# Encoder layer on one core: two sums of weight blocks added by the DMA queues, and eight fused pairs instead of six in three of four output groups

## The chip, the cores and the metric

The kernel runs on one core of a Trainium2 chip. A run's time is the device time of one execution, in microseconds (us). The profile comes from one execution, recorded by the hardware profiler. Its engines are TensorE (PE; the loading of its weights is PEld), VectorE (DVE), ScalarE (ACT), GpSimd (POOL) and SyncE (SP), each with an instruction queue of its own; DMAs are issued by SP, ACT or POOL.

## The reference, cut to what matters

One layer on 256 positions with 4096 channels: a normalised input times a wide matrix, a convolution path and an attention path beside each other, each with a gate, and an output projection whose result is added to the input.

```python
xn = rms_norm(x, norm_g)
h = xn @ w_in                                   # 4096 -> 14336
c_val, c_glu, c_gate, q, k, v, a_gate = split(h)
conv_out = conformer_conv(c_val, c_glu, ...) * silu(c_gate)
attn_out = longnet_mixture(rms(q), rms(k), v, rel_bias) * silu(a_gate)
mixed = concatenate([conv_out, attn_out])       # 256 x 4096
x = x + mixed @ w_out                           # 4096 -> 4096, the stage that changes
```

## The kernel before, in words

Every matrix product is made of three products in a 32-bit format of lower precision. Each operand is split into a high part (ScalarE rounds it) and a low part (VectorE subtracts the high part from the original). Then high x high, low x high and high x low are added up in PSUM. In the input stage these are L662, L663 and L665, in the output stage L782, L783 and L784 (in `triple`).

The work goes in groups of 1024 output columns: 14 input groups and four output groups (`og` 0 to 3). Along the inner dimension a group has 16 pairs `j`, each of two blocks `k` of 128 rows. The weights of a pair, 128 partitions x 2048 numbers, come by one DMA of 1 MB on SP's queue into one of three `raw` tiles (`load_pair`, L190). When the weights of pair `u` have been split, the load of pair `u + 3` is issued; SP waits until the slot is free.

An output group multiplies the mixed activations (256 rows, as two halves `s`) by two column halves `e`. A pair has therefore 2 x 2 blocks of activations, `a11` to `a22`, and 2 x 2 blocks of weights, `b11`, `b12`, `b21`, `b22`. There are two ways to work off a pair.

- A plain pair (`plain`) makes all 8 block products, each of 3 matmuls of 512 columns.
- A fused pair (`fused`) uses a Strassen-like scheme with 7 block products. It needs sums of blocks on both sides. On the activations these are `s1` to `s4`, made once (`mix_fuse`, called by `mix_split_gen`) and kept in a tile `mx` for all four groups. On the weights they are `t1` to `t4`, made anew for every pair in `split_fused`. The seven products go into `c11`, `c12`, `c21` and into `m1`, `m5`, `m6`, `m7`; the `m` banks are added to the output once per group (`add_more`).

`split_fused` has four steps. `one` makes the tile t13 = (t1, t3) on VectorE (L748) and splits b11 and b21. `two` rounds t13 on ScalarE (L732), starts t24 on VectorE (L759) and makes t13's low part (L736). `three` makes the other half of t24 (L765) and splits b22 (L767, L736). `four` splits t24. Each step asks for one or two tiles for its results. `before` lets steps run as long as no more than 8 such tiles are held, 10 after slot 10 of the first group, so the splits run ahead of TensorE by about that much.

The order of the pairs in a group is written out by hand:

```python
FUSED = (0, 1, 2, 3, 4, 5)
OUT_ORDERS = [(8, 9, 10, 0, 6, 1, 11, 2, 7, 3, 12, 4, 13, 5, 14, 15)]
OUT_ORDERS += 3 * [(8, 9, 0, 10, 1, 11, 2, 6, 3, 7, 4, 12, 5, 13, 14, 15)]
```

Pairs 0 to 7 are attention channels, 8 to 15 convolution channels. The convolution channels are multiplied by their gate late (L416), the last of them while the first output group already runs. `mix_split_gen` then splits or sums them (L547, L548, L559 to L571). All this side work is emitted by `pump`, step by step, with a budget of declared VectorE and ScalarE cost per call.

Tiles of 4 KB per partition share the pool tag `c4` with 15 slots: activations, gates, the `mx` tiles, t13, t24, the residual `xr` and split results beyond the eight `ws` slots. An instruction that writes such a tile waits until the slot's last user is done.

At the start seven small matmuls on a constant (`spin`, L900) run before the first weights have landed.

Of the kernel before, what the change touches and what calls it, by code (L numbers as in the profile page):

```python
# [17 lines left out]
P = 128  # L18
# [93 lines left out]
def layer_kernel(  # L112
# [17 lines left out]
    def t4(name):  # L130
        return sb.tile([P, 4, 256], F32, tag="c4", bufs=15, name=name)

# [44 lines left out]

    raw_tiles = {}

    def load_pair(j, cuts=(0, 2048), between=None):  # L180

        g, jj = divmod(j, n_pairs)
        if g >= NG:
            return
        if groups[g][0] == "out":
            jj = (OUT_ORDERS[g - n_in][jj] + n_pairs // 2) % n_pairs
        rt = sb.tile([P, 2048], F32, tag="raw", bufs=RAW, name=f"raw{j}")
        raw_tiles[j] = rt.rearrange("p (k c) -> p k c", k=2)
        for lo, hi in zip(cuts, cuts[1:]):
            nc.sync.dma_start(rt[:, lo:hi], w[g, jj, :, lo:hi])  # L190
            if between and hi == 1024:
                between()
# [335 lines left out]
    def mix_split_gen():  # L528
        waiting, done = list(OUT_ORDERS[0]), 0
        while waiting:  # L530
            for j in waiting:
                if 2 * j in mix_ready and 2 * j + 1 in mix_ready:
                    break
            else:
                yield
                continue
            while progress["in"] < done + 3:
                yield
            waiting.remove(j)
            done += 2  # L540
            if j in FUSED:
                yield from mix_fuse(j)
                continue
            for kk in (2 * j, 2 * j + 1):
                h, l = new_split(kk, "m")
                src = mix_ready[kk]
                nc.scalar.copy(h, src)  # L547
                nc.vector.tensor_sub(l, src, h.bitcast(F32))  # L548
                mh[kk], ml[kk] = h, l
                yield 335  # L550

    def mix_fuse(j):
# [4 lines left out]
        sums = t2(f"mix_sums{j}")  # L557
        s1, s2, s3, s4 = (sums[:, P * i : P * i + P] for i in range(4))
        nc.vector.tensor_add(s1, a21, a22)  # L559
# [5 lines left out]
        b0, b1 = new_split(2 * j, "m"), new_split(2 * j + 1, "m")  # L565
        more = sb.tile([P, 2, 512], F32R, tag="c4", bufs=15, name=f"mx{j}")
        parts = [[b[:, :P] for b in b0], [b[:, P:] for b in b0], b1]
        parts.append([more[:, i, : 3 * P] for i in range(2)])
        for (h, l), src in zip(parts, (a11, s1, a1, sums[:, P:])):
            nc.scalar.copy(h, src)  # L570
            nc.vector.tensor_sub(l, src, h.bitcast(F32))  # L571
            yield 300, 300
        names = {"a11": parts[0], "s1": parts[1]}
        names["a12"] = [b[:, :P] for b in b1]
        names["a22"] = [b[:, P:] for b in b1]
        for i in range(3):
            names[f"s{i + 2}"] = [more[:, hl, P * i : P * i + P] for hl in range(2)]
        mx[j] = names
# [93 lines left out]
    class Out:  # L672
# [3 lines left out]
        def __init__(self):  # L676
# [5 lines left out]
            for u in range((NG - n_in) * n_pairs):  # L682
                og, slot = divmod(u, n_pairs)
                j = OUT_ORDERS[og][slot]
                make = self.split_fused if j in FUSED else self.split_plain
                self.todo.extend((n, f, u) for n, f in make(u))

        def tile(self, name, of):
# [3 lines left out]
            self.tags.setdefault(of, []).append(tag)  # L692
            bufs = W_SLOTS if tag == "ws" else 15
            return sb.tile([P, 1024], F32R, tag=tag, bufs=bufs, name=name)
# [27 lines left out]
        def split_fused(self, u):  # L722
# [19 lines left out]
            def one():  # L742
                r = raw_tiles[n_in * n_pairs + u].rearrange("p k (e c) -> p (k e) c", e=2)
                kept["r"] = r
                t13 = kept["t13"] = t4(f"t13_{u}").rearrange("p a b -> p (a b)").rearrange(
                    "p (a c) -> p a c", a=2
                )
                nc.vector.tensor_sub(t13, r[:, 1:4:2, :], r[:, 0:2, :])  # L748
                h, l = both("b", r[:, 0:3:2, :])
                low(h, l, r[:, 0:3:2, :])  # L750
                keep(("b11", "b21"), h, l)

            def two():
                r, t13 = kept["r"], kept["t13"]
                t24 = kept["t24"] = t4(f"t24_{u}").rearrange("p a b -> p (a b)").rearrange(
                    "p (a c) -> p a c", a=2
                )
                h, l = both("t13", t13)
                nc.vector.tensor_sub(t24[:, 0, :], r[:, 3, :], t13[:, 0, :])  # L759
                low(h, l, t13)  # L760
                keep(("t1", "t3"), h, l)

            def three():
                r, t24 = kept["r"], kept["t24"]
                nc.vector.tensor_sub(t24[:, 1, :], r[:, 2, :], t24[:, 0, :])  # L765
                hl = halves("b22s", "b22")
                nc.scalar.copy(hl[:, 0, :], r[:, 3, :])  # L767
                low(hl[:, 0, :], hl[:, 1, :], r[:, 3, :])
                self.parts[(u, "b22")] = (hl[:, 0, :], hl[:, 1, :])

            def four():
                h, l = both("t24", kept["t24"])
                low(h, l, kept["t24"])
                keep(("t2", "t4"), h, l)
# [19 lines left out]
        def group(self, og):  # L794
# [3 lines left out]
            more = None  # L798
            fused_left = len(FUSED)
            for slot, j in enumerate(OUT_ORDERS[og]):  # L800
                u = og * n_pairs + slot
                self.settled |= slot == 10
                if slot == 9:
                    for e in range(2):
# [4 lines left out]
                        xr_tiles[(g, e)] = t  # L809
                if j in FUSED:  # L810
# [4 lines left out]
                    first, last = fused_left == len(FUSED), fused_left == 1  # L815
                    self.fused(u, j, one, more, first, last)
# [57 lines left out]
        def add_more(self, g, more):  # L874
# [8 lines left out]
            nc.vector.tensor_add(v, u, more["m7"])  # L883
            for dst, src in ((r[0][0], m1), (r[0][1], u), (r[1][0], v), (r[1][1], v)):
                nc.vector.tensor_add(dst, dst, src)

# [11 lines left out]
    spin = side("spin")  # L898
    for _ in range(7):
        nc.tensor.matmul(spin[:, :P], ones, ones, start=True, stop=True)  # L900
# [107 lines left out]
```

## Time and profile before

| | before |
|---|---|
| median of 3 runs | 1603.34 us (1603.1 to 1603.47) |
| the profiled execution, its time | 1603.12 us |
| its span, first to last instruction | 1601.3 us |
| mean granted TensorE clock | 0.998 |
| matmul rows | 6986 |
| busy: TensorE, VectorE, ScalarE, GpSimd | 1590.5, 1195.0, 968.2, 0.2 us |
| read from HBM | 318.08 MB |
| output groups in the span | 1257.76 us to the end |

A row of a timeline reads: start and length in us, engine, line of the kernel, operation, the tile written and the tiles read, shape, count. Brackets hold the idle time of the engine before it and what ended that. A row of waits reads: engine and line that waited, for whom; us in total, times, longest. A row of groups reads: line, engine, operation, tiles, shapes, count; busy us, mean ns of one; idle us before them. Matmul records overlap, so their pace is read from their starts, or from a count over a stretch.

### The profile page before, as it was taken

The numbers are of one execution on the slowest core, as the hardware profiler recorded it, in microseconds if no ns is written. First come the engines' busy times: TensorE is split into PE (matmuls) and PEld (weight loads), VectorE is DVE, ScalarE is ACT, GpSimd is POOL, SyncE is SP. The second block draws the span as 40 slices with busy tenths as digits, with TensorE's granted clock in tenths as the row PEclk, the third lists the DMA queues.
The fourth block names the chain that finished last, engine by engine and source line by source line (L and its number), as shares of the span: only waits on it lengthen the run. The fifth ranks groups of instructions, "written<-read, shape, count | busy, mean of one in ns | idle before, by whom it ended". The sixth has DMA issues, their size and how long they took to land.

```text
span 1601.3 us, 18984 instructions
## 1 busy us (share of the span) xinstructions
PE 1590.5 (99%) x6986; PEld 1312.8 (82%) x6986; DVE 1195.0 (75%) x1630; ACT 968.2 (60%) x1480; POOL 0.2 (0%) x4
## 2 busy tenths in 40 slices
PE   9999999999999999999999999999999999999999
PEld 7888888888888888888888888888878877888887
DVE  6668888888888887678755556555467889888886
ACT  6763534445453467755779557754789865545453
POOL 0000000000000000000000000000000000000000
PEclk9999999999999999999999999999999999999999
DMA  9755555555555555555555555455545556665653
GB/s 377 289 184 198 196 186 201 192 184 207 188 190 204 184 195 191 186 186 191 179 195 189 192 203 190 173 187 207 194 163 190 184 210 232 232 229 215 248 198 143
DMA packets 52892, 323.53 MB, mean 202 GB/s; under 512 B 5792, under 2 KB 8480, under 8 KB 16192
## 3 DMA queue, kind: packets, MB, share of 16 engines
q1 hardware_dynamic: 52512, 322.05, 56.4%
q8 instruction: 54, 0.88, 0.2%
q10 hardware_dynamic: 288, 0.28, 0.1%
q14 instruction: 38, 0.31, 0.1%
HBM read 318.08 MB, written 4.23 MB: 201 GB/s over the span
## 4 chain that ended last, share of the span: by engine, by line
PE 96%; ACT 1%; DVE 1%; issue 0%; DMA 0%; DVEq 0%; ACTq 0%
PE acc L662 25%; PE acc L663 25%; PE acc L665 25%; PE c L784 5%; PE c L782 5%; PE c L783 5%; PE m L784 1%; PE m L782 1%; PE m L783 1%; PE po L514 1%; PE psc L475 1%; ACT gate L315 0%; ACT pr L505 0%; DMA first_x<-in_x_cols_dram 0%; DVE t24l L736 0%
## 5 line engine op out<-in xcount | busy, mean ns | idle before, releaser
L205 DVE TENSOR_TENSOR wl<-raw,wh 128x1024 fp32r<-128x1024 f32 x447 | 546.9, 1224 | 336.9 <-ACT wh L204 335.9
L204 ACT CAST wh<-raw 128x1024 fp32r<-128x1024 f32 x447 | 469.6, 1052 | 434.9 <-PE acc L663 241.5
L662 PE MATMUL acc<-wh,xh 128*128 128x512 f32 x1792 | 703.8, 393 | 1.3 <-ACT xh L252 1.3
L663 PE MATMUL acc<-wh,xl 128*128 128x512 f32 x1792 | 698.4, 390 | 0.0
L665 PE MATMUL acc<-wl,xh 128*128 128x512 f32 x1792 | 483.7, 389 | 0.0
L662 PEld LDWEIGHTS acc<-wh,xh 128*128 128x128 f32 x1792 | 337.0, 188 | 72.3 <-ACT xh L252 1.6
L663 PEld LDWEIGHTS acc<-wh,xl 128*128 128x128 f32 x1792 | 336.8, 188 | 70.1 <-DVE xl L253 0.2
L665 PEld LDWEIGHTS acc<-wl,xh 128*128 128x128 f32 x1792 | 336.3, 188 | 70.3
L346 DVE SCALAR_TENSOR_TENSOR cT<-conv,wT,cT 128x241 f32<-128x241 f32 (+14 forms) x480 | 201.6, 471 | 0.0
L782 PE MATMUL c<-oh,mh 128*128 128x512 f32 x320 | 125.3, 391 | 0.5 <-ACT oh L716 0.5
L784 PE MATMUL c<-ol,mh 128*128 128x512 f32 x320 | 125.1, 391 | 0.5 <-DVE ol L717 0.5
L783 PE MATMUL c<-oh,ml 128*128 128x512 f32 x320 | 125.0, 391 | 0.0
L716 ACT CAST oh<-raw 128x1024 fp32r<-128x1024 f32 x80 | 83.2, 1051 | 50.8 <-PE c L783 34.4
L717 DVE TENSOR_TENSOR ol<-raw,oh 128x1024 fp32r<-128x1024 f32 x80 | 96.1, 1222 | 21.8 <-ACT oh L716 15.2
L505 ACT COPY pr<-turn_p 32x128 f32<-32x128 f32 x256 | 75.9, 297 | 9.2 <-DVE turn_p L499 5.7
L782 PEld LDWEIGHTS c<-oh,mh 128*128 128x128 f32 x320 | 60.5, 189 | 13.5 <-ACT oh L716 1.0
L784 PEld LDWEIGHTS c<-ol,mh 128*128 128x128 f32 x320 | 60.3, 189 | 13.5 <-DVE ol L717 1.0
L783 PEld LDWEIGHTS c<-oh,ml 128*128 128x128 f32 x320 | 60.5, 189 | 12.8
L732 ACT CAST t24h<-t 128x1024 fp32r<-128x1024 f32 x24 | 25.2, 1051 | 40.3 <-PE c L783 24.1
L736 DVE TENSOR_TENSOR t24l<-t,t24h 128x1024 fp32r<-128x1024 f32 x24 | 29.4, 1226 | 17.3 <-ACT t24h L732 17.3
L732 ACT CAST t13h<-t 128x1024 fp32r<-128x1024 f32 x24 | 25.3, 1053 | 18.2 <-DVE t L748 14.2
L732 ACT CAST bh<-raw 128x1024 fp32r<-128x1024 f32 x24 | 25.3, 1053 | 16.3 <-PE m L783 16.3
(195 smaller groups left out, 1030.8 us busy)
## 6 DMA issues: line engine op xcount, KB each, us to landing
raw<-in_w_dram SPq DMA_DIRECT2D x286, 1024.0 KB, 4.8
x<-in_x_dram SPq DMA_DIRECT2D x8, 512.0 KB, 7.4
xr<-in_x_dram SPq DMA_DIRECT2D x8, 512.0 KB, 6.0
out_dram<-xr SPq DMA_DIRECT2D x15, 256.0 KB, 2.9
xT<-in_x_cols_dram SPq DMA_DIRECT2D x7, 512.0 KB, 6.9
T<-bias_dram SPq DMA_DIRECT2D x16, 192.0 KB, 5.0
raw<-in_w_dram SPq DMA_DIRECT2D x3, 512.0 KB, 6.2
raw<-in_w_dram SPq DMA_DIRECT2D x2, 256.0 KB, 4.4
```

The source lines that it names most:

```text
L204: nc.scalar.copy(wh, src)
L205: nc.vector.tensor_sub(wl, src, wh.bitcast(F32))
L346: nc.vector.scalar_tensor_tensor(c[:, t, lo:hi], a[:, t, lo + sh : hi + sh], wT[:, ch, k : k + 1], c[:, t, lo:hi], op0=ALU.mult, op1=ALU.add,)
L505: nc.scalar.copy(dst[32 * b : 32 * b + 32, :, :, 3 - a, :], backwards(blocks[32 * a : 32 * a + 32, :, :, b, :]),)
L662: nc.tensor.matmul(a, hs, wp, start=k == 0, stop=False)
L663: nc.tensor.matmul(a, ls, wp, start=False, stop=False)
L665: nc.tensor.matmul(a, hs, wp, start=False, stop=k == KT - 1)
L716: nc.scalar.copy(h, src)
L717: nc.vector.tensor_sub(l, src, h.bitcast(F32))
L782: nc.tensor.matmul(acc, a[0], b[0], start=start, stop=False)
L783: nc.tensor.matmul(acc, a[1], b[0], start=False, stop=False)
L784: nc.tensor.matmul(acc, a[0], b[1], start=False, stop=stop)
```

## The change

- Groups two to four have eight fused pairs (0 to 7), the first group keeps six; the orders of groups two to four are new.
- The weight sums change sign, so that they are plain sums: t1 = b11 + b12, t3 = b12 + b22, t2 = t1 + b22, t4 = t2 + b21. The signs in `mix_sums` and `add_more` follow.
- t13 is no longer made by VectorE. `load_pair` loads (b11, b12) into the tile by SP and adds (b12, b22) to it by an accumulating DMA on POOL's queue. Block b12 is not loaded into `raw` for a fused pair; the rest of it comes by two DMAs.
- t24 is made in place in t13's tile, in the third step.
- All pairs get plain splits of their activations; the fused pairs' sums follow, those of pairs 6 and 7 after all the others. The declared costs in `mix_split_gen` change.
- The `c4` pool gets 18 slots instead of 15, and the scratch that the DMA queues of POOL reserve in each partition is set to 2048 bytes.
- Eleven spinning matmuls instead of seven.

```diff
-FUSED = (0, 1, 2, 3, 4, 5)
+FUSED = [range(6)] + 3 * [range(8)]
-OUT_ORDERS += 3 * [(8, 9, 0, 10, 1, 11, 2, 6, 3, 7, 4, 12, 5, 13, 14, 15)]
+OUT_ORDERS += 3 * [(8, 9, 0, 10, 1, 11, 2, 3, 12, 4, 5, 13, 6, 7, 14, 15)]
+C4 = 18
...
         rt = sb.tile([P, 2048], F32, tag="raw", bufs=RAW, name=f"raw{j}")
         raw_tiles[j] = rt.rearrange("p (k c) -> p k c", k=2)
+        if fuse:
+            src = w[g, jj].rearrange("p (k e c) -> p k e c", k=2, e=2)
+            t = sums[j] = t4(f"t13_{j}").rearrange("p a b -> p (a b)").rearrange(
+                "p (a c) -> p a c", a=2
+            )
+            nc.sync.dma_start(t, src[:, 0])
+            nc.gpsimd.dma_start(t, src[:, :, 1], accum_op=ALU.add)
+            nc.sync.dma_start(rt[:, 0:512], w[g, jj, :, 0:512])
+            nc.sync.dma_start(rt[:, 1024:2048], w[g, jj, :, 1024:2048])
+            return
...
-            if j in FUSED:
-                yield from mix_fuse(j)
-                continue
             for kk in (2 * j, 2 * j + 1):
                 h, l = new_split(kk, "m")
...
-                yield 335
+                yield 400, 400
+            if j in FUSED[0]:
+                yield from mix_sums(j)
+        for j in FUSED[-1]:
+            if j not in mx:
+                yield from mix_sums(j)
...
+        nc.vector.tensor_sub(s1, a21, a22)
         nc.vector.tensor_sub(s2, s1, a11)
-        yield 400
+        yield 580
         nc.vector.tensor_sub(s3, a11, a21)
-        nc.vector.tensor_sub(s4, a12, s2)
-        yield 400
+        nc.vector.tensor_add(s4, a12, s2)
+        yield 580
+        parts = sb.tile([P, 2, 512], F32R, tag="c4", bufs=C4, name=f"mx{j}")
+        nc.scalar.copy(parts[:, 0], t)
+        nc.vector.tensor_sub(parts[:, 1], t, parts[:, 0].bitcast(F32))
+        yield 690, 620
...
             def one():
-                nc.vector.tensor_sub(t13, r[:, 1:4:2, :], r[:, 0:2, :])
+                kept["r"], kept["t"] = r, sums.pop(j)
...
             def two():
                 h, l = both("t13", t)
-                nc.vector.tensor_sub(t24[:, 0, :], r[:, 3, :], t13[:, 0, :])
                 low(h, l, t)
...
             def three():
-                nc.vector.tensor_sub(t24[:, 1, :], r[:, 2, :], t24[:, 0, :])
                 hl = halves("b22s", "b22")
                 nc.scalar.copy(hl[:, 0, :], r[:, 3, :])
+                nc.vector.tensor_add(t[:, 0, :], t[:, 0, :], r[:, 3, :])
+                nc.vector.tensor_add(t[:, 1, :], t[:, 0, :], r[:, 2, :])
                 low(hl[:, 0, :], hl[:, 1, :], r[:, 3, :])
...
-    for _ in range(7):
+    for _ in range(11):
         nc.tensor.matmul(spin[:, :P], ones, ones, start=True, stop=True)
...
-    nc = _bacc.Bacc("TRN2", target_bir_lowering=False, num_devices=1)
+    nc = _bacc.Bacc("TRN2", target_bir_lowering=False, num_devices=1, dynamic_dma_scratch_size=2048)
```

More of the change, by code (lines that the diff above doesn't have):

```diff
@@ L549, in mix_split_gen, with mix_sums @@
                 mh[kk], ml[kk] = h, l
[L550 to L552 removed]
+                yield 400, 400
[4 more added lines that the diff above has]
+                yield from mix_sums(j)
+    def mix_sums(j):
         a0, a1 = mix_ready[2 * j], mix_ready[2 * j + 1]
         a11, a21, a12, a22 = a0[:, :P], a0[:, P:], a1[:, :P], a1[:, P:]
[L557 to L559 removed]
+        t = t2(f"mix_sums{j}")
+        s1, s2, s3, s4 = (t[:, P * i : P * i + P] for i in range(4))
+        nc.vector.tensor_sub(s1, a21, a22)
         nc.vector.tensor_sub(s2, s1, a11)
[L561 removed]
+        yield 580
         nc.vector.tensor_sub(s3, a11, a21)
[L563 to L577 removed]
+        nc.vector.tensor_add(s4, a12, s2)
[4 more added lines that the diff above has]
+        yield 690, 620
+        names = {
+            f"s{i + 1}": [parts[:, hl, P * i : P * i + P] for hl in range(2)] for i in range(4)
+        }
+        names["a11"] = [m[2 * j][:, :P] for m in (mh, ml)]
+        names["a12"] = [m[2 * j + 1][:, :P] for m in (mh, ml)]
+        names["a22"] = [m[2 * j + 1][:, P:] for m in (mh, ml)]
         mx[j] = names
@@ L771, in four @@
             def four():
-                h, l = both("t24", kept["t24"])
-                low(h, l, kept["t24"])
+                h, l = both("t24", kept["t"])
+                low(h, l, kept["t"])
                 keep(("t2", "t4"), h, l)
```

40 lines of the change are left out of this document (19 added, 21 removed).

## The prediction

> **What bounds the kernel now.** I read the page's head first, then the stages by windows, then TensorE's waits, then a timeline where it waits.
>
> ```profile
> PE 1590.5 (99%) x6986; PEld 1312.8 (82%) x6986; DVE 1195.0 (75%) x1630; ACT 968.2 (60%) x1480; POOL 0.2 (0%) x4
> ...
> 300.00:600.00 300.00, 300.00 (x1325) 248.43 (x1324) 255.27 (x415) 148.04 (x183) 0.00 (x0) 1.00 0.55 193
> ...
> 1257.70:1342.90 85.20, 81.61 (x344) 64.72 (x344) 75.59 (x104) 60.69 (x97) 0.00 (x0) 0.98 0.54 198
> 1348.30:1431.30 83.00, 83.00 (x368) 68.70 (x367) 72.19 (x78) 42.78 (x46) 0.00 (x0) 1.00 0.69 245
> ```
>
> The window rows read: stretch and its length, busy time and count of PE, of weight loads, DVE, ACT and POOL, then granted clock, DMA share and GB/s. TensorE is the bound: 1325 matmuls in 300 us without a gap, 0.2264 us each. So what TensorE need not do is gained, wherever it has no gap. The third row is nearly all of the first output group: 344 matmuls would take 77.9 us and took 85.2, so 7.3 us are lost there. The fourth row is the second group: 368 matmuls at that pace are 83.3 us, nothing is lost. The loss in the first group has a reason that the waits and a timeline show.
>
> ```profile
> PE m L782 <- ACT t24h L732: 1.2, 1, 1.2
> PE m L784 <- DVE t24l L736: 1.1, 3, 0.5
> ...
> 1281.57 1.22 DVE L748 TENSOR_TENSOR t<-raw 128x1024 f32<-128x1024 f32 x1
> ...
> 1290.20 1.23 DVE L736 TENSOR_TENSOR t24l<-t,t24h 128x1024 fp32r<-128x1024 f32 x1 [0.52 <-ACT t24h L732]
> ...
> 1290.22 0.50 PE L782 MATMUL m<-t24h,mx 128*128 128x512 f32 x1 [1.22 <-ACT t24h L732]
> ...
> 1292.75 0.63 PE L782 MATMUL c<-oh,mh 128*128 128x512 f32 x1
> 1293.18 0.63 PE L783 MATMUL c<-oh,ml 128*128 128x512 f32 x1
> ...
> 1293.00:1296.00 3.00, 3.00 (x9) 2.32 (x9) 3.00 (x4) 1.05 (x2) 0.00 (x0) 0.56 0.32 87
> ```
>
> TensorE waits for the last parts of a fused pair, t24, because VectorE (75.6 us busy of 85.2) is behind: from L748 at 1281.57 to the t24l at 1290.20 it works nearly without a gap, gate and mix work in between. The wait has a second price: right behind it matmuls start 0.43 us apart, and the granted clock is 0.56 in 1293 to 1296.
>
> **The change part by part.** The profiled execution took 1603.12 us (span 1601.3); the median is 1603.34, 0.22 above. The sum is made on 1603.12.
>
> *Matmuls.* A fused pair issues 7 products of 3 matmuls, a plain one 8 of 3. Fused pairs go from 6 in each of four groups to 6, 8, 8, 8: six more, 18 matmuls fewer, 18 x 0.2264 = 4.08 us. Groups two to four have no gap, so all of it counts: **-4.1**.
>
> *VectorE loses L748; the two t24 sums stay (now both in the third step, in place).*
>
> ```profile
> L736 DVE TENSOR_TENSOR t24l<-t,t24h 128x1024 fp32r<-128x1024 f32 x6 | 7.4, 1226 | 4.1 <-ACT t24h L732 4.1
> ...
> L748 DVE TENSOR_TENSOR t<-raw 128x1024 f32<-128x1024 f32 x6 | 7.3, 1218 | 0.0
> ...
> L759 DVE TENSOR_TENSOR t<-raw,t 128x512 f32<-128x512 f32 x6 | 4.1, 684 | 0.0
> ...
> L548 DVE TENSOR_TENSOR ml<-cT,mh 128x256 fp32r<-128x256 f32 x8 | 3.4, 422 | 0.5
> ...
> L571 DVE TENSOR_TENSOR mx<-mix_sums,mx 128x384 fp32r<-128x384 f32 x3 | 1.6, 541 | 0.5 <-ACT mx L570 0.5
> L571 DVE TENSOR_TENSOR ml<-mix_sums,mh 128x128 fp32r<-128x128 f32 x3 | 0.9, 290 | 1.1 <-ACT mh L570 1.1
> ...
> L559 DVE TENSOR_TENSOR mix_sums<-agv 128x128 f32<-128x128 f32 x2 | 0.6, 280 | 0.0
> ...
> 1282.70 1.22 DVE L736 TENSOR_TENSOR bl<-raw,bh 128x1024 fp32r<-128x1024 f32 x1
> ```
>
> These are VectorE's groups of the first output group. L748 costs 1.22 us, but the next operation starts 1.13 after it (1281.57 to 1282.70), so 1.13 is gained per fused pair: 6.8 us in the first group, 5.7 of it ahead of the last stall. Against it: the mix work. For a fused pair the low parts were two of 128 columns, one of 256, one of 384 (2 x 0.29 + 0.42 + 0.54 = 1.54); now they are two of 256 and one of 512 (2 x 0.42 + 0.68 = 1.52), and the four sums of 128 stay: nothing. But pairs 6 and 7, plain in the first group, now need sums as well: 2 x (4 x 0.28 + 0.68) = 3.6 us. They are emitted after all other mix work, behind the worst of it. Their pacing costs also rise (from 2000 to 2650 declared per fused pair), so some mix work moves from the input stage into this group. If VectorE paces this group, 7.3 us of loss fall by 5.7 less some 1 to 2 of moved mix work, and the slow-clock part (9 matmuls in 3 us around 1294 lack 1.0 us) goes with the wait that made it. Ends: 0 (ScalarE or the order of emission is late next) and -7.3. I take **-4.0**, nearer to VectorE's own count because the wait for t24h ends on it. Late next is t24l behind t24h, which already has 4.1 us of idle before it.
>
> In groups two to four two or three fused pairs in a row cost VectorE 3 lows of 1.13 and 3 halves of 0.6, 5.2 us, against 21 x 0.2264 = 4.75 of TensorE; each plain pair between gives 3 us back. Before, 6.3 and 5.4 alternated without a gap. Nothing, covered by the lead of the splits.
>
> *The sum t13 comes by two DMAs.* A load by SP, then, when it has landed, an accumulating one by POOL; ScalarE's t13h waits for the second. The raw load loses a quarter and splits in two. Per fused pair 1.75 MB replace 1 MB.
>
> ```profile
> raw<-in_w_dram SPq DMA_DIRECT2D x286, 1024.0 KB, 4.8
> x<-in_x_dram SPq DMA_DIRECT2D x8, 512.0 KB, 7.4
> xr<-in_x_dram SPq DMA_DIRECT2D x8, 512.0 KB, 6.0
> out_dram<-xr SPq DMA_DIRECT2D x15, 256.0 KB, 2.9
> ...
> SPq L190 <- DVE ol L717: 153.7, 35, 6.9
> SPq L190 <- DVE b22s L736: 105.2, 22, 7.9
> ...
> 1373.13 14.82 SPq L190 DMA_DIRECT2D raw<-in_w_dram  x4
> ...
> 1382.35 1.05 ACT L732 CAST bh<-raw 128x1024 fp32r<-128x1024 f32 x1 [1.48 <-PE m L783]
> ...
> 1383.63 1.05 ACT L732 CAST t13h<-t 128x1024 fp32r<-128x1024 f32 x1 [0.23 <-DVE t L748]
> ```
>
> A load of the second group is issued at 1373.13, as its slot comes free; its first cast is at 1382.35, its t13h at 1383.63, 10.5 us after issue. The new chain is a load (4.8 at most for this size) plus the accumulation A, which no row shows. Its nearest row is xr, 512 KB in the same shape: 6.0 (ends: 2.9, a quieter queue; 12, if reading the destination doubles it). 4.8 + 6.0 = 10.8 against 10.5. But SP waits about 4.5 us ahead of each load (153.7/35) for the raw slot alone, and the sum's own tile is not a raw slot, so its load, first of the pair's in SP's order, can go out right behind the pair before, up to those 4.5 us earlier. And the splits run ahead of TensorE, so a single delay is covered. I take **0**, plus **+0.3** for a few first uses. POOL has nothing else to do (0.2 us in all). SP issues two more DMAs per fused pair, under 1 us of its 4.5 of waiting.
>
> *Traffic.* Twelve slots with eight fused pairs last 8 x 4.75 + 4 x 5.43 = 59.7 us and load 18 MB of weights and 2 of residual and output: 21.0e6 bytes, 351 GB/s; 422 if accumulation counts double.
>
> ```profile
> 20.00:30.00 10.00, 10.00 (x45) 8.26 (x44) 7.24 (x10) 6.81 (x13) 0.00 (x0) 1.00 1.03 410
> ```
>
> At the start the queues carried 410 GB/s. So the plain count fits and the doubled one lacks 2 us in a group, which the four plain slots at its ends give back: 0. A rule of the Trainium skill (DMA: Bandwidth & Descriptors, Specifications) speaks against the change: it gives about 358 GB/s as a core's share of HBM. By that, the doubled count would need 70 us for 59.7. This trace's 410 is over it, so I stay with the row.
>
> *Eleven spins instead of seven.*
>
> ```profile
> 1.04 3.36 PE L900 MATMUL spin<-ones 128*128 128x128 f32 x14 [1.04 <-DVE ones L143]
> 5.73 0.80 PE L662 MATMUL acc<-wh,xh 128*128 128x512 f32 x1 [1.33 <-ACT xh L252]
> ...
> 8.13 0.63 PE L663 MATMUL acc<-wh,xl 128*128 128x512 f32 x1
> ...
> 8.90 0.39 PE L663 MATMUL acc<-wh,xl 128*128 128x512 f32 x1
> ...
> 14.39 1.05 ACT L204 CAST wh<-raw 128x1024 fp32r<-128x1024 f32 x1 [2.08 <-DMA raw<-in_w_dram]
> ...
> 16.86 0.39 PE L662 MATMUL acc<-wh,xh 128*128 128x512 f32 x1
> ```
>
> Seven spins are 14 rows, 0.24 us each; then 1.33 idle; then seven matmuls take 3.17 us (5.73 to 8.90) where 0.2264 each would be 1.58. Four more spins fill the gap: eight rows, 1.9 us, to 6.3 at the slow pace, a delay of 0.6. If the clock is granted by then, 1.6 are gained, of which ScalarE's cast at 15.44 (behind a DMA) lets some 1.4 through to the matmul at 16.86. Ends -1.4 and +0.6; I take **-0.9**, as the later gap and recovery at 1293 show that the clock follows how busy TensorE was. The Trainium skill (TensorE: Matmul & The Clock Gate, What's actually happening) says that full rate comes after one busy window of about 3.4 us whose phase is not the kernel's; by it, I estimate full rate between 4.5 and 7.9 us, and a gain near 0.8 after the delay. The trace agrees as far as 3.36 us of spins did not do it.
>
> *Smaller DMA scratch, 18 slots in c4, other signs.* Nothing by themselves: they make room, and the same number of adds remains.
>
> Sum: 1603.1 - 4.1 - 4.0 + 0.3 - 0.9 = 1594.4 for an execution as profiled, 1594.6 at the median.
>
> **The rivals.**
>
> *A: the accumulated sum is late (slower).* Three raw slots make a ring: load, accumulate, then t13h to the end of t24l.
>
> ```profile
> 1374.35 1.06 ACT L732 CAST t13h<-t 128x1024 fp32r<-128x1024 f32 x1 [1.15 <-PE c L784]
> ...
> 1378.89 1.23 DVE L736 TENSOR_TENSOR t24l<-t,t24h 128x1024 fp32r<-128x1024 f32 x1 [0.57 <-ACT t24h L732]
> ```
>
> That last part is 5.8 us. Two fused pairs and a plain one are 14.9 us on TensorE. The ring holds it up when 4.8 + A + 5.8 is over 14.9 + 4.5, the head start: A over 8.8 us. With A = 12, each round lacks 3.2, some four rounds in each of four groups, 51 us, less the splits' lead of up to 7.5 in each: about 20. 1594.6 + 20 = 1615. For it: accumulation has no row, and queues will be twice as full as in the 6.0. Against it: 6.0 is well under 8.8.
>
> *B: only the matmuls count.* The first group's loss stays because ScalarE's chain or the slower mix pacing takes VectorE's place: 1603.3 - 4.1 - 0.9 + 0.3 = 1598.6. For it: t24l waits for t24h there already. Against it: VectorE 89% busy in that window.
>
> *C: SP's queue stops in the first group.* The sum's load needs a c4 slot while gate, convolution and attention tiles still hold theirs; pairs 6 and 7 now hold an attention tile to the end of the mix work, and two of the three new slots go to their mix tiles.
>
> ```profile
> 1288.36 0.42 DVE L416 TENSOR_TENSOR cT<-cT,gate 128x256 f32<-128x256 f32 x1
> ...
> 1314.69 0.42 DVE L416 TENSOR_TENSOR cT<-cT,gate 128x256 f32<-128x256 f32 x1
> ```
>
> Between these two gate products none frees a tile, 26.3 us. A load that comes to a full pool half-way waits 13.2, and the raw loads behind it too; less 4.5 of head start, 8.7 are put back: 1603.3, no change. It decides from 16 or more tiles held at once. Against it: sums and splits free their own slots every pair.
>
> **How the numbers follow.** Forecast 0.56, its own range 1590 to 1597. B 0.17, A 0.17, C 0.10. Faster by over 0.2% (3.2 us, about what a measurement of this kernel can tell from no change) holds the forecast and nearly all of B: 0.73. Within: C, a mild A: 0.09. Slower: the rest of A and a bad C, 0.18. The low end, 1589.5, is the sum with the first group's whole 7.3 and 1.4 at the start gone (1590.5), and 1 us less for rounding in these; the high end, 1606, takes in B, C and the mildest of A (A of 9.5 us) and leaves its worse forms out.
>
> **What would show it.** Matmul rows are 6986 - 18 + 8 (spins) = 6976. L748 is gone; a POOL DMA appears 30 times, landing in about 6 us. The window of the first group shows under 4 us lost and no clock under 0.9; those of groups two to four PE busy throughout; the eighth matmul behind the spins starts before 8.5 us. Wrong would be: PE waits for t13h in groups two to four with ScalarE waiting for a DMA (A), SP waiting for the t load in the first group (C), or 7 us lost there still (B).

## The result and the profile after

The changed kernel takes 1628.65 us (median of four runs, 1625.05 to 1634.33) against 1603.33 us before: the ratio is 1.0161, 95% interval 1.0132 to 1.0191. (A ratio here is an estimate over all executions and need not be the quotient of the two medians.) It is 25 us slower, where 1594.6 was forecast; the range ended at 1606. The profiled execution took 1628.34 us with a span of 1626.5.

First the page's head, its DMA queues and its DMA issues.

```profile
PE 1599.4 (98%) x6976; PEld 1305.9 (80%) x6976; DVE 1191.2 (73%) x1634; ACT 974.4 (60%) x1488; POOL 33.1 (2%) x34
...
q1 hardware_dynamic: 61152, 329.92, 56.7%
q0 software_dynamic: 8160, 15.73, 5.7%
...
raw<-in_w_dram SPq DMA_DIRECT2D x33, 512.0 KB, 6.7
t<-in_w_dram SPq DMA_DIRECT2D x30, 512.0 KB, 7.8
t<-in_w_dram POOLq DMA_DIRECT2D x30, 512.0 KB, 7.9
```

The 6976 matmuls are those that were counted. The sum's two transfers land 7.8 and 7.9 us after their issue, in the median. Queue q0 holds the 30 accumulating DMAs and nothing else. Its 15.73 MB take 5.7% of the 16 engines' span, 0.36% for each MB; q1's 329.92 MB take 56.7%, 0.17% for each. So an accumulated byte occupies the DMA engines about twice as long as a loaded one: 170 GB/s of busy time (15.73 MB by 5.7% of 1626.5 us) against 358.

Then the four output groups by windows (length, busy and count of PE, weight loads, DVE, ACT and POOL, granted clock, DMA share, GB/s).

```profile
1257.26:1350.32 93.06, 87.63 (x368) 68.47 (x366) 78.25 (x114) 63.16 (x97) 6.82 (x7) 0.98 0.80 240
1350.32:1440.26 89.94, 85.49 (x361) 66.72 (x360) 70.03 (x77) 44.63 (x50) 8.76 (x8) 1.00 0.92 280
1440.26:1529.97 89.71, 85.26 (x362) 66.71 (x360) 70.01 (x77) 44.66 (x50) 8.75 (x8) 1.00 0.93 282
1529.97:1622.60 92.63, 85.95 (x361) 66.45 (x359) 69.36 (x77) 40.98 (x46) 7.67 (x7) 1.00 0.81 239
```

The first group issues 366 of these products, the others 360 (six fused pairs of 21 and ten plain ones of 24; then eight of each; a window's count holds one or two of its neighbour). At 0.2266 us each, measured between matmul starts in a stretch without gaps, that is 82.9 and 81.6 us. So the groups lose 10.1, 8.4, 8.1 and 11.1 us, 37.7 in all. The same count on the trace of before gives 7.6 in the first group and nothing in the others. There the first and the third group, of 366 products each, were:

```profile
1257.76:1348.33 90.57, 86.98 (x367) 69.20 (x366) 80.96 (x110) 62.42 (x99) 0.00 (x0) 0.98 0.53 194
...
1431.29:1514.25 82.96, 82.96 (x367) 68.69 (x366) 70.15 (x74) 43.04 (x46) 0.00 (x0) 1.00 0.63 228
```

All of the added time is here: +30.0 of gaps, -4.1 of matmuls, -0.5 ahead of the first group make +25.4, where the profiled executions differ by 25.2. "Losses" below always means this count, in the profiled execution.

What ends the gaps is in the waits (waiting engine, tile and line, what came last; total, times, longest).

```profile
DVE t13l L749 <- ACT t13h L745: 44.0, 18, 6.8
ACT t13h L745 <- DMA t<-in_w_dram: 35.2, 15, 6.0
...
PEld m L791 <- DVE t24l L749: 13.4, 15, 1.0
PEld m L791 <- DVE t13l L749: 7.0, 9, 1.0
...
PE m L789 <- ACT t13h L745: 4.5, 5, 1.1
...
SPq L198 <- PE c L790: 2.1, 5, 0.6
```

ScalarE's t13h waits for the sum's DMA 15 times. In 19 of the 30 fused pairs t13h starts within 0.1 us of its accumulation's landing. VectorE's low part, then TensorE, wait behind it. One such pair, the second of group two, in the timeline:

```profile
1351.83 3.07 SPq L621 DMA_DIRECT2D out_dram<-xr  x4
...
1354.94 0.53 SPq L198 DMA_DIRECT2D t<-in_w_dram  x1
1355.57 0.59 SPq L200 DMA_DIRECT2D raw<-in_w_dram  x1
...
1359.51 0.38 SPq L198 DMA_DIRECT2D t<-in_w_dram  x1
...
1362.58 1.11 POOL L199 DMA_DIRECT2D t<-in_w_dram  x1 [13.94 <-DVE ol L730]
...
1363.73 0.33 SPq L200 DMA_DIRECT2D raw<-in_w_dram  x1
...
1364.67 1.05 ACT L745 CAST bh<-raw 128x1024 fp32r<-128x1024 f32 x1 [2.22 <-DMA raw<-in_w_dram]
...
1372.70 1.04 ACT L745 CAST t13h<-t 128x1024 fp32r<-128x1024 f32 x1 [6.97 <-PE c L790]
...
1373.80 0.50 PE L789 MATMUL m<-t13h,mx 128*128 128x512 f32 x1 [0.88 <-ACT t13h L745]
1374.14 0.39 PE L790 MATMUL m<-t13h,mx 128*128 128x512 f32 x1
1375.06 0.50 PE L791 MATMUL m<-t13l,mx 128*128 128x512 f32 x1 [0.53 <-DVE t13l L749]
...
1377.11 0.50 PE L791 MATMUL c<-b22s,mx 128*128 128x512 f32 x1 [0.39 <-DVE b22s L749]
...
1378.90 0.50 PE L791 MATMUL m<-t24l,mx 128*128 128x512 f32 x1 [0.53 <-DVE t24l L749]
```

SP issues the load at 1354.94, behind the four stores of the output group just finished. POOL issues the accumulation at 1362.58, and it lands at 1372.62: 17.7 us from the first issue. ScalarE stands idle for 6.97 us ahead of t13h. The row names PE's release of the tile, but the cast starts 0.08 us behind the landing; the raw parts were there 8 us earlier (bh at 1364.67). Then each of the pair's parts comes late in turn: TensorE waits 0.88, 0.53, 0.39 and 0.53 us and starts matmuls 0.34 apart behind a wait. The pair loses 3.8 us; the same pair of the next two groups loses 3.5 and 3.9. These three make 11.2 of the 27.6 us that groups two to four lose; pairs 5 to 7, late in each group, make nearly all of the rest (16.2).

At the start, the extra spins bring TensorE's full pace forward:

```profile
1.06 4.27 PE L909 MATMUL spin<-ones 128*128 128x128 f32 x22 [1.06 <-DVE ones L144]
5.48 0.50 PE L675 MATMUL acc<-wh,xh 128*128 128x512 f32 x1 [0.16 <-ACT xh L266]
...
6.35 0.40 PE L675 MATMUL acc<-wh,xh 128*128 128x512 f32 x1
6.58 0.40 PE L676 MATMUL acc<-wh,xl 128*128 128x512 f32 x1
...
7.50 0.39 PE L676 MATMUL acc<-wh,xl 128*128 128x512 f32 x1
```

The first product starts at 5.48 (5.73 before) and the eighth at 7.50 (8.90 before).

### The profile page after: what moved, and what is told of

Read it like the earlier page. It is cut to its first block, busy times and chain, and to the rows that moved or that the text cites. A ratio compares the mean times of both kernels' runs of the same rounds, so it can differ in the third digit from the quotient of the medians.

```text
span 1626.5 us, 19221 instructions
## 1 busy us (share of the span) xinstructions
PE 1599.4 (98%) x6976; PEld 1305.9 (80%) x6976; DVE 1191.2 (73%) x1634; ACT 974.4 (60%) x1488; POOL 33.1 (2%) x34
## 3 DMA queue, kind: packets, MB, share of 16 engines
q1 hardware_dynamic: 61152, 329.92, 56.7%
q0 software_dynamic: 8160, 15.73, 5.7%
## 4 chain that ended last, share of the span: by engine, by line
PE 86%; DMA 7%; DVE 4%; ACT 2%; issue 1%; SPq 0%; ACTq 0%; DVEq 0%; POOLq 0%
PE acc L675 25%; PE acc L676 25%; PE acc L678 24%; DMA t<-in_w_dram 6%; PE c L789 3%; PE c L790 3%; PE c L791 3%; PE po L528 1%; PE psc L489 1%; PE m L791 1%; DVE t24l L749 1%; DVE t13l L749 1%; DMA raw<-in_w_dram 1%; ACT t24h L745 1%; DVE ol L730 1%
## 5 line engine op out<-in xcount | busy, mean ns | idle before, releaser
L791 PE MATMUL c<-ol,mh 128*128 128x512 f32 x272 | 106.0, 390 | 0.5 <-DVE ol L730 0.5
L789 PE MATMUL c<-oh,mh 128*128 128x512 f32 x272 | 106.0, 390 | 0.3 <-ACT oh L729 0.3
L790 PE MATMUL c<-oh,ml 128*128 128x512 f32 x272 | 105.9, 389 | 0.0
L730 DVE TENSOR_TENSOR ol<-raw,oh 128x1024 fp32r<-128x1024 f32 x68 | 80.5, 1219 | 4.8 <-ACT oh L729 3.3
L729 ACT CAST oh<-raw 128x1024 fp32r<-128x1024 f32 x68 | 68.5, 1047 | 19.3 <-PE c L790 8.8
L749 DVE TENSOR_TENSOR t13l<-t,t13h 128x1024 fp32r<-128x1024 f32 x30 | 36.7, 1222 | 44.0 <-ACT t13h L745 44.0
L199 POOL DMA_DIRECT2D t<-in_w_dram x30 | 33.0, 1098 | 1562.6 <-ACT gate L639 1255.9
L791 PEld LDWEIGHTS c<-ol,mh 128*128 128x128 f32 x272 | 51.1, 188 | 11.6 <-DVE ol L730 1.0
L789 PEld LDWEIGHTS c<-oh,mh 128*128 128x128 f32 x272 | 51.1, 188 | 11.4 <-ACT oh L729 0.7
L790 PEld LDWEIGHTS c<-oh,ml 128*128 128x128 f32 x272 | 51.1, 188 | 10.7
```

The costliest lines, as they stand in the source:

```text
L789: nc.tensor.matmul(acc, a[0], b[0], start=start, stop=False)
L790: nc.tensor.matmul(acc, a[1], b[0], start=False, stop=False)
L791: nc.tensor.matmul(acc, a[0], b[1], start=False, stop=stop)
```

## The experiments

Three theories were set against each other. L: the sum's load is issued too late, hardly ahead of the pair's own raw parts, and a chain of two transfers from there is too long. Q: the transfers themselves are too long, by the accumulation's price and by full queues, whenever they start. V: VectorE, in the order or the number of its mix operations. The first four kernels below shared one chip and its runs of the kernel before (median 1603.1), the next four another set (1603.43), the last two a third (1603.09). A loss belongs to one execution, which can lie off the median: 3.4 us above it for the copies, 2.1 for the sums one pair earlier, 2.0 for these with the old costs, 1.1 for six pairs everywhere, 1.6 below it for the stores, and 0.3 or less for all others.

**Six fused pairs in every group, sums by DMA.** This undoes the fused pairs' number and order, and keeps the accumulation.

```diff
-FUSED = [range(6)] + 3 * [range(8)]
+FUSED = 4 * [range(6)]
-OUT_ORDERS += 3 * [(8, 9, 0, 10, 1, 11, 2, 3, 12, 4, 5, 13, 6, 7, 14, 15)]
+OUT_ORDERS += 3 * [(8, 9, 0, 10, 1, 11, 2, 6, 3, 7, 4, 12, 5, 13, 14, 15)]
```

> The changed kernel, but with six fused pairs in all four groups in the order of before: the sums by DMA alone. In the changed kernel t13h waits for the accumulating DMA, whose landing takes 5.6 us in a quiet stretch and up to 12 in a full one. Theory Q (queues: the DMA queues are near what they can carry, because the sums need 0.75 MB more per fused pair and an accumulation takes them longer per byte): with 24 sums that alternate with plain pairs the queues empty in between; groups two to four lose 1 to 3 us each instead of 8 to 11, the first group its 10: 1609 to 1614. Theory L (chain: two DMAs in series are too long for the head start, full queues or not): each sum is as late as before, groups two to four lose 6 to 8 each: 1624 to 1630. Theory V (eight fused pairs, two in a row, are too much for VectorE and ScalarE): no loss outside the first group: 1604 to 1606.

Measured: 1621.08 us, ratio 1.0116 (1.0101 to 1.0131). The groups lose 7.0, 8.1, 5.9 and 6.2. From its waits:

```profile
ACT t13h L745 <- DMA t<-in_w_dram: 60.3, 12, 7.6
```

Even where no two fused pairs follow each other, the sum is late, by up to 7.6 us. So the density of fused pairs is a smaller part: V's figure is far off. The time lies between Q's and L's, nearer to L's 1624, and the losses of groups two to four are close to those that L expected (6 to 8).

**Eight fused pairs, sums by VectorE.** This is the other half: no accumulation at all.

```diff
+BY_DMA = 4 * [()]
...
-            fuse = OUT_ORDERS[g - n_in][jj] in FUSED[g - n_in]
+            fuse = OUT_ORDERS[g - n_in][jj] in BY_DMA[g - n_in]
...
-                kept["r"], kept["t"] = r, sums.pop(j)
+                t = sums.pop(j, None)
+                if t is None:
+                    t = ...
+                    nc.vector.tensor_add(t, r[:, 0:2, :], r[:, 1:4:2, :])
+                kept["r"], kept["t"] = r, t
```

> The changed kernel with its eight fused pairs, its orders, spins and slots, but every t13 made by VectorE from a full raw load, as before: the eight pairs alone. Theories Q and L: no sum is late. VectorE has 2 x 6.3 + 2.3 = 14.9 us for two fused pairs and a plain one, TensorE 14.9: groups two to four lose 0 to 2 us each, the first group 7 to 9 as before; 1603.3 - 4.1 - 0.8 = 1598.4, up to 1604. Theory V: groups two to four lose 8 us or more each as in the changed kernel: 1622 or more.

Measured: 1614.2 us, ratio 1.0071 (1.0056 to 1.0086); the expectation of 1598 to 1604 missed by 10 us. The groups lose 13.0, 4.2, 3.2 and 3.3. Without the accumulation groups two to four lose 10.7 instead of 27.6, so the sums by DMA cost 17 us more there than VectorE's own. But VectorE does not carry eight fused pairs for nothing either: pairs 5 and 7, which follow another fused pair, lose 1 to 2 us each. And the first group is far worse than before (13.0 against 7.6). Its window, and VectorE's timeline at its worst place:

```profile
1257.23:1353.13 95.90, 88.38 (x368) 69.05 (x366) 86.78 (x122) 63.16 (x97) 0.00 (x0) 0.98 0.51 187
```

```profile
1328.73 0.28 DVE L576 TENSOR_TENSOR mix_sums<-agv 128x128 f32<-128x128 f32 x1
...
1337.37 0.69 DVE L584 TENSOR_TENSOR mx<-mix_sums,mx 128x512 fp32r<-128x512 f32 x1 [0.68 <-ACT mx L583]
1338.32 1.23 DVE L750 TENSOR_TENSOR t24l<-t,t24h 128x1024 fp32r<-128x1024 f32 x1 [0.25 <-ACT t24h L746]
```

Between 1328.73 and 1338.06 VectorE works, among other things, on the activation sums of pairs 6 and 7, which no product of this group reads, and the low part t24l of the last fused pair comes behind them.

**Copies in place of accumulation.** POOL's DMA writes its block over the tile; the sum of the two blocks is left out, everything else stays.

```diff
-            nc.gpsimd.dma_start(t, src[:, :, 1], accum_op=ALU.add)
+            nc.gpsimd.dma_start(t, src[:, :, 1])
```

> The changed kernel, but the DMA on POOL's queue copies the second blocks over the first instead of adding them (the sums are left out); queue, bytes from HBM, waits and order are the same. Theory Q, if the accumulation's longer time on the queues is the larger part: landing of POOL's DMA falls from a median of 7.9 us to under 6.5, losses fall by half or more: 1603 to 1614. Theory Q, if the 0.75 MB more are the larger part, and theory L: 1622 to 1629, landing as long as before.

Measured: 1609.19 us, ratio 1.0041 (1.0026 to 1.0056). The groups lose 6.6, 5.3, 5.4 and 4.3, 21.6 in all against 37.7. Its queue and its issues:

```profile
q0 software_dynamic: 4320, 15.73, 2.9%
...
t<-in_w_dram POOLq DMA_DIRECT2D x30, 512.0 KB, 6.0
```

The same bytes from the same engine take half the share and land in 6.0 us. So the doubled occupancy comes with the adding. It is not the size of the packets alone, although the accumulation moves 2 KB in each where the copies move 4: in the trace of the changed kernel a packet of 2 KB takes 178 ns on q0 and 84 ns on q1, in the median. The time and the landing are what Q expected of a costly accumulation (1603 to 1614, under 6.5 us); L's 1622 to 1629 is missed. In groups two to four 27.6 us of loss become 15.0, in an execution 3.4 us above the median. So about half of the loss comes with the adding. The rest remains with two plain transfers one behind the other (15.6 us in the median, where the changed kernel has 17.8), which speaks for L.

**The sum's two DMAs one pair earlier.** The pair's sum is requested ahead of the raw tile of the pair before it, with one more slot to hold it.

```diff
-C4 = 18
+C4 = 19
...
         rt = sb.tile([P, 2048], F32, tag="raw", bufs=RAW, name=f"raw{j}")
+        load_sum(j + 1)      # the sum's tile and its two DMAs, taken out of this function
...
         if fuse:
-            t = sums[j] = ...
-            nc.sync.dma_start(t, src[:, 0])
-            nc.gpsimd.dma_start(t, src[:, :, 1], accum_op=ALU.add)
```

> The changed kernel, but the sum of the next pair is loaded and accumulated ahead of the raw load of a pair, so one pair (about 5 us) earlier; one more c4 slot (19) holds it. Same bytes, same operations. Theory L: 5 us more head start are more than the waits of 0.1 to 7 us at t13h in most pairs: the losses of groups two to four fall from 8 to 11 us each to 0 to 2, 1602 to 1609. Theory Q: the queues carry the same bytes in the same time; the raw loads come later in exchange, and the loss falls by less than half: 1614 to 1630. Theory V: no change, 1628.

Measured: 1598.57 us, ratio 0.9975 (0.9965 to 0.9986): 30 us less than the changed kernel, 4.5 us less than before, and 3 us below the range that L gave, which did not count on the first group's gain (10.1 to 6.6). The groups lose 6.6, 2.0, 0.0 and 1.1. The same pair as above in its timeline, then group three by windows, then the DMA view of that stretch:

```profile
1340.47 0.42 SPq L190 DMA_DIRECT2D t<-in_w_dram  x1
...
1348.54 3.35 SPq L628 DMA_DIRECT2D out_dram<-xr  x4
...
1362.69 1.05 ACT L752 CAST t13h<-t 128x1024 fp32r<-128x1024 f32 x1
```

```profile
1430.59:1512.19 81.60, 81.60 (x361) 67.57 (x360) 70.43 (x77) 45.22 (x50) 8.76 (x8) 1.00 0.98 312
```

```profile
q1 hardware_dynamic: 5865, 21.47, 71.0%
q0 software_dynamic: 2038, 3.92, 26.8%
```

The load goes out 8 us ahead of the stores instead of behind them, and this t13h waits for nothing. In the whole kernel nine of the 30 still start as their sum lands (19 in the changed kernel). Group three runs without a gap although its DMA engines are busy 98% of the time, and although the sum's chain, from its load's issue to the accumulation's landing, is not shorter: 18.6 us in the median, 17.8 in the changed kernel. So with a chain of this length it is the start that decides, as L says; full queues alone cost nothing in this group. The added slot is hardly the cause: in the changed kernel SP waited 3 us in all for a tile of the sum.

**Output stores of groups one to three on POOL's queue.**

```diff
-                                (nc.scalar, nc.sync) if end else (nc.sync,))
+                                (nc.scalar, nc.sync) if end else (nc.gpsimd if g < NG - 1 else nc.sync,))
```

> The changed kernel, but the four output stores of groups one to three are issued on POOL's queue instead of SP's. In the changed kernel the sum's load of the second fused pair of groups two to four stands behind these stores in SP's order, and they wait for VectorE's last adds (last store 1353.80, that load 1354.94); this pair then loses 3.8, 3.5 and 3.9 us. If the head start lost in SP's order is the cause there, these three losses fall to under 1 each and the rest stays: 1616 to 1620. If only full queues count (the stores' bytes stay), no change: 1625 to 1630.

Measured: 1620.1 us, ratio 1.0111 (1.0096 to 1.0126), at the end of the expected 1616 to 1620. The second fused pair of groups two to four loses 1.8, 1.2 and 1.6 instead of 3.8, 3.5 and 3.9, where under 1 each was expected. More than half of that loss was SP's queue, less than all. The same pair as above:

```profile
1349.64 0.49 SPq L198 DMA_DIRECT2D t<-in_w_dram  x1
1353.92 0.33 SPq L200 DMA_DIRECT2D raw<-in_w_dram  x1
...
1369.86 1.05 ACT L745 CAST t13h<-t 128x1024 fp32r<-128x1024 f32 x1 [5.68 <-DMA t<-in_w_dram]
```

Its load now goes out with the start of its group (1349.51) and 4.3 us ahead of the raw part. In the changed kernel it went out 4.6 us behind the start of the group. But the two transfers took 8.3 and 11.1 us instead of 7.0 and 10.0, which is Q's part, and t13h gains only 2 us of it. The groups together lose 27.3 instead of 37.7; the 3.8 us that these three pairs do not explain are spread over the others.

**Early, with the mix work's old declared costs.** The edit is on top of the early kernel's.

```diff
-                yield 400, 400
+                yield 335
...
-        yield 580
+        yield 400
...
-        yield 580
+        yield 400
...
-        yield 690, 620
+        yield 300, 300
```

> The kernel with sums a pair earlier (which lost 6.6 us in the first group and 3.1 in the others), with the declared costs of the mix work set back to those of before (335 per split, 400 for two sums, 300 and 300 for the sums' split). With VectorE's sums the first group lost 13.0 us, where the kernel before lost 7.6. If the slower declared pace moved mix work into the first group and costs the 5 us between these, the first group's loss falls from 6.6 to 1 to 4, and the time to 1593 to 1597. If the difference comes from the two more mix sums and the order, no change: 1598 to 1600.

Measured: 1599.67 us, ratio 0.9979 (0.997 to 0.9988), beside 1598.57 of the early kernel on another set. The first group loses 7.2, against 6.6: no change, and the time lies in the range given for that. The declared costs are not what holds it up.

**Early, and in groups two to four only pairs 3, 5 and 7 by DMA**, the ones that follow another fused pair; VectorE adds the rest, by the lines of the second experiment. The edit is on top of the early kernel's.

```diff
+BY_DMA = [range(6)] + 3 * [(3, 5, 7)]
```

> The kernel with sums a pair earlier, but in groups two to four only pairs 3, 5 and 7 (the second of two fused pairs in a row) have their sum by DMA, the other five by VectorE. Theory Q (full queues lengthen both DMAs): POOL's DMA lands in 5.5 to 7 us instead of 9.4 and no t13h waits for it. VectorE has 13.8 us of work for 14.9 of TensorE in two fused pairs and a plain one: groups two to four lose 0 to 1 each, the first 6.6: 1595 to 1598. If VectorE's load is what leaves the 3.1 us now, they lose 3 or more each: 1600 to 1606.

Measured: 1597.93 us, ratio 0.9967 (0.9954 to 0.9979), in the range that Q gave. The losses are 6.6, 0.4, 0.4 and 0.1. Group two by windows, and the issues:

```profile
1346.88:1428.86 81.98, 81.94 (x362) 67.49 (x360) 75.57 (x82) 44.59 (x50) 3.29 (x3) 1.00 0.78 260
```

```profile
t<-in_w_dram SPq DMA_DIRECT2D x15, 512.0 KB, 5.7
t<-in_w_dram POOLq DMA_DIRECT2D x15, 512.0 KB, 6.5
```

In the early kernel they were:

```profile
t<-in_w_dram SPq DMA_DIRECT2D x30, 512.0 KB, 8.9
t<-in_w_dram POOLq DMA_DIRECT2D x30, 512.0 KB, 9.4
```

At a DMA share of 0.78 instead of 0.98 the two transfers land in 5.7 and 6.5 us instead of 8.9 and 9.4: Q's part, the length of the transfers, follows the load on the queues. Of the 3.1 us of gaps in groups two to four 0.8 are left. But the early kernel's 3.1 is from an execution 2.1 us above its median, and the two medians, each less that of its own set's kernel before, differ by 1 us (-5.5 and -4.5).

**Eleven spins alone**, in the kernel before.

```diff
-    for _ in range(7):
+    for _ in range(11):
```

> The kernel before with eleven spins instead of seven, nothing else. In the changed kernel the first output group began 0.5 us earlier than before (1257.26 against 1257.76), of 0.9 forecast. If the spins made all of this: 1602.6 to 1603.0, a ratio of 0.9997; if the forecast holds, 1602.4.

Measured: 1602.39 us against 1603.43, ratio 0.9996 (0.9987 to 1.0005). Its span is 1600.6 against 1601.3. The interval does not tell the gain from zero. In the trace the eighth product starts at 7.45 and the first output group at 1257.05, 0.7 us earlier than before. In the eleven profiled kernels with eleven spins that group starts at 1256.99 to 1257.66, so 0.1 to 0.8 earlier.

**Sums by VectorE, with the activation sums of pairs 6 and 7 held back to slot 14 of the first group.** The edit is on top of the second experiment's.

```diff
+        while progress.get("out", 0) < 14:
+            yield
         for j in FUSED[-1]:
             if j not in mx:
...
-                u = og * n_pairs + slot
+                u = progress["out"] = og * n_pairs + slot
```

> The eight fused pairs with all sums by VectorE, but the activation sums of pairs 6 and 7 are emitted only from slot 14 of the first output group on. There these sums stood in VectorE's order in front of the low parts of pair 5, and the first group lost 13.0 us where the kernel before lost 7.6. If they are the cause, the loss falls by their 3.4 to 5 us, to 8 to 9.6: 1609 to 1611 (it was 1614.2). If the t24 sum that moved to the third step is the cause, no change in the first group's loss: 1613 to 1615.

Measured: 1612.24 us, ratio 1.0058 (1.0044 to 1.0071), 1.2 above the expected range. The first group falls as expected, from 13.0 to 8.3. But the second rises from 4.2 to 6.9: 0.9 of it at its first fused pair, right behind the sums, and most of the rest (1.6) at pair 3. The work was moved, and more than half of the gain paid back.

**Both: early, pairs 3, 5 and 7 by DMA, late activation sums.** The edits are those above, together.

```diff
+BY_DMA = [range(6)] + 3 * [(3, 5, 7)]
-C4 = 18
+C4 = 19
...
+        load_sum(j + 1)
...
+        while progress.get("out", 0) < 14:
+            yield
```

> Sums a pair earlier, by DMA for all six pairs of the first group and for pairs 3, 5 and 7 of the others, and the activation sums of pairs 6 and 7 from slot 14 of the first group on. Without the last edit the first group lost 6.6 us, 1.8 of it at pair 5, whose low parts stand behind these sums. If they are the cause there, its loss falls to 4.8 to 5.2 and the time from 1597.9 to 1595.5 to 1596.5; otherwise it stays at 1597 to 1598.5.

Measured: 1597.27 us (1597.23 to 1597.91), ratio 0.9965 (0.9952 to 0.9979). The losses are 4.8, 1.9, 0.3 and 0.0: again the first group falls (from 6.6), as expected, and the second gives 1.5 back. So the time is not in the range that the cause promised (1595.5 to 1596.5) but in the other. It has the lowest time of all, 6 us under the kernel before, but its interval overlaps with that of the kernel without the late sums. What is left in its first group is not VectorE's alone. At the second fused pair, which loses 1.9, the sum t24 is done at 1285.71, but:

```profile
1286.68 0.41 ACT L566 CAST mh<-cT 128x256 fp32r<-128x256 f32 x1 [2.20 <-DVE cT L438]
1286.99 1.04 ACT L755 CAST t24h<-t 128x1024 fp32r<-128x1024 f32 x1
```

ScalarE's t24h stands behind a mix split that waits for VectorE's gate product, and TensorE waits 0.8 us for it.

## Why the prediction was wrong, step by step

*The step that failed: "I take 0, plus +0.3" for the sum by two DMAs.* Groups two to four lost 27.6 us instead. It went wrong in three ways.

First, the sizes. The load was put at 4.8 us "at most" and took 7.8; the accumulation at 6.0 and took 7.9. With POOL's issue between them (0.7 us from the load's landing in the median), the chain has a median of 17.8 us (12.1 to 21.6) where 10.8 stood against a lead of 10.5. The 4.8 was a median over the whole run, most of it at a DMA share of 0.55, where these groups have 0.92. The prediction knew that ("queues will be twice as full"), but applied it to the accumulation's rival alone. Rival A's threshold, A over 8.8, was not met by the median of A (7.9), though 13 of the 30 were above it. The sum behind it, 4.8 + 8.8 = 13.6 us, was exceeded by 27 of the 30 chains, because the load lengthened too.

Second, the head start. "Right behind the pair before, up to those 4.5 us earlier" is what SP's order gives in the middle of a group: one pair later in the timeline shown, the load goes out at 1359.51 and its raw part at 1363.73. But SP's queue also holds the output stores, and there the start was 0.6 us (1354.94 and 1355.57). The stores' rows were in the trace of before; what is queued ahead of the new load was not followed. This accounts for the second fused pair of groups two to four alone, and moving the stores away gave back 6.6 of its 11.2 us. The early kernel shows the whole step: a chain as long, but started one pair sooner, brings 27.6 down to 3.1.

Third, the traffic. "The plain count fits" rested on one row of 410 GB/s at a share of 1.03, from the kernel's first 30 us. The prediction's other rows said less: 193 GB/s at 0.55 and 245 at 0.69 make 351 and 355 GB/s for a full queue. After the change q1 again makes 358 (371 in group three of the early kernel). And the doubled count, which was set aside, is what q0 shows. A group's 25.46 MB with the 3.92 accumulated ones counted twice are 29.4 MB. At 358 GB/s that is 82.1 us, for 81.6 us of TensorE: the queues are all but full, as the early kernel's 0.98 shows. That lengthens the two transfers; it is no loss of its own. A single window at the start of a run is not a rate to plan with. The Trainium skill (DMA: Bandwidth & Descriptors, Specifications), which the prediction set aside, gives about 358 GB/s as a core's share of HBM. The average here agrees with that figure; what sets it, no run here shows.

*"VectorE loses L748", -4.0.* The mechanism was right and bigger than forecast, but the other side of it was misplaced. Taking the sums from VectorE in a first group with otherwise the same work brings its loss from 13.0 (sums by VectorE) to 6.6 (early), -6.4, where 5.7 were counted. Against it, "behind the worst of it" is refuted: the 3.6 us of activation sums for pairs 6 and 7 stand ahead of the last fused pair's t24l, and holding them back took 4.7 us off with VectorE's sums, 1.8 with the sums by DMA. The slower declared costs, put at 1 to 2 us, were worth nothing that these runs show (7.2 with the old ones, 6.6 with the new). So the step takes the loss from 7.6 to 6.6: -1.0 instead of -4.0. In the changed kernel itself it is +2.5 (10.1), since one sum is late there too: the fifth fused pair's accumulation took 11.5 us and the pair lost 4.6, against 1.1 in the early kernels.

*Matmuls, -4.1.* Right: 6976 rows, and in the early kernel group three takes 81.60 us against 82.96 before, 1.36 for six matmuls.

*Fused pairs in a row in groups two to four, "nothing, covered by the lead of the splits".* With the sums on VectorE this costs 10.7 us, so as a rule about the fused pair it does not hold. With the sums off VectorE it was right: 0.0 in group three of the early kernel.

*Spins, -0.9.* The eighth product starts 1.40 earlier, as the signature asked (before 8.5). Of that 0.5 is left at the first output group (1257.26 against 1257.76), which lies between the ends given; the other profiled kernels with eleven spins keep 0.1 to 0.8, and run by itself the gain is not told from zero. By the Trainium skill's rule of one busy window of about 3.4 us (TensorE: Matmul & The Clock Gate, What's actually happening), the estimate was full rate between 4.5 and 7.9 us and a gain near 0.8. The trace agrees: starts are 0.23 us apart from 6.35 on, which lies in that span.

*The rivals.* A happened, at a chance of 0.17, by the load and the accumulation together rather than by A alone, and in groups that lost 30 us more where 20 were worked out. Its signature (t13h waits for a DMA in groups two to four) is what the waits show. C did not: SP waited for the sum's load 3 us in the whole run, in waits of 0.6 at most. B's remaining 7 us in the first group is close to what the early kernel has there (6.6). Of these, 1.8 are the activation sums on VectorE. No run takes the other 4.8 apart; the timeline of the last kernel shows ScalarE's order in a part of them, which is B's reason.

## What to carry to other kernels

Work that is moved from an engine to the DMA queues becomes a chain of landings, and a prefetch distance tuned for one landing has to be set again: here groups two to four lost 28 us with the same two transfers when they started with their pair, and 3 us when they started a pair earlier. Work out the chain with landings at the load the queues will have, and with everything that stands ahead of the new DMA in its issuing queue. Convert the rate from many windows as GB/s by share before saying that traffic fits, and put only as many sums on the queues as the engine cannot do: half of them gave the same time with a fifth of the queues free.

## What the runs showed of the hardware

An accumulating DMA occupied the DMA engines twice as long for each byte as a plain one: 5.7% against 2.9% of the span for the same 15.73 MB from the same queue, and 178 ns against 84 for a packet of 2 KB. Its landing time was no constant: 5.6 us at the least and 12.0 at the most in one execution (that of the changed kernel). And DMA engines that were 98% busy, for 81.6 us, did not slow TensorE in that stretch, where the sums had been asked for some 20 us ahead of their use (22 in the pair shown, 1340.47 to 1362.69).
